# Attention of an encoder block in an order from estimated times, outputs of two query blocks at a time, the second norm's factor behind its product

## The chip, the cores and the metric

The kernel runs on one core of a Trainium2 chip. A core has five engines with a queue of instructions each: TensorE (PE) multiplies matrices into PSUM, VectorE (DVE), ScalarE (ACT) and GpSimd (POOL) do the elementwise work, SyncE (SP) issues DMAs. An engine takes its instructions in their order; semaphores hold one until what it needs is there. The metric is the time of one execution on the device in microseconds; the time before is the median of three runs.

## The reference

One layer on a sequence of 1024 frames with 1024 features, in float32:

```
h   = rmsnorm(x); q, k, v of groups A and B = split(h @ w_in)      # 8 heads of 64 each
ya  = softmax(q k^T / 8 + bias) v       # own chunk of 64 frames and the 8 before it
z   = q k^T / 8                         # group B: stick breaking, strictly causal
a   = exp(log_sigmoid(z) + sum of log(1 - sigmoid(z)) over the keys between)
yb  = a v
x   = x + concat(rmsnorm(ya), rmsnorm(yb)) @ w_out
x   = x + (silu(conv3(gate)) * conv3(value)) @ w_ffn_out            # gate|value = rmsnorm(x) @ w_ffn_in
out = rmsnorm(x)
```

## The kernel before

**Precision.** Each float32 operand of a large product is split into a high part and a low rest, and three products (high x high, high x low, low x high) are added in PSUM: `mm3` (L138 to L145). The split costs a cast on ACT and a subtraction on DVE or GpSimd.

**Stages.** From 0 to 58 us the input is normed and q, k and v of the first head pair are made. Attention of group B follows (58 to 355 us), then that of group A (355 to 540 us; the second half of the output projection begins inside it), the rest of that projection with the second norm's beginning (to 600 us), and the feed-forward part to the end. Heads go in pairs, n = 0 to 3 in group B and 4 to 7 in group A (there p = n - 4).

**Group B** (`BlockB`, L385 on). For each pair of heads and query block i of 128 frames there are KT - i key blocks; the order of frames is reversed, so block 0 is the widest with 8. `scores` writes z (`zb`) into one of two PSUM buffers of two banks each; two sigmoids on ACT, a scan and a product on DVE (L410 to L415) follow. `turn` transposes the result by key blocks (`tpb`, L423) and ACT copies it to SBUF. `output` (L433) multiplies by v with half of the array's columns per head, (`yb`), and DVE copies the sums (L437). Block b's scores, block b-2's transposes and an output in between make one turn of the loop (L667 to L701).

**Group A** (`BlockA`, L451 on) does the same with a softmax: bias (L482), maximum (L484), exponential with its sum (L492), reciprocal (L493), shares (L494), transposes (`tpa`), outputs (`yy`, L521), and a copy into a quarter of `yq`. Each four blocks the result is scaled and split for the output projection (L536, L537) and squared.

**The filler.** Projections of later head pairs (`q`, `k`, `v`) and the group B half of the output projection (`pb`) are a generator, whose pieces of three matmuls are put between the pieces of attention at fixed rates (RATE_B, RATES_A, `run`). Before the first block of a head pair, `need` finishes the projections it lacks.

**What sets the order.** The order on PE is the program's. On DVE, ACT, GpSimd and SP a scheduler puts the instructions in order by a simulated timeline until the second half of the output projection; from there on (`own_order`, `loads_order`, L843 to L846) these are in program order too. PSUM buffers in question: two banks `pj` for projections, two banks `med` for transposes, outputs and sums, two pairs `big` for scores.

**Second norm of attention.** The outputs of group B are spilled to memory as they are; their squares are summed, and `prepare_b` loads them again, multiplies by gain and factor (L547) and splits them for `pb`. The product is added to x directly (L577). For group A the factor is applied behind the product (`paf`, L575).

Of the kernel before, what the change touches and what calls it, by code (L numbers as in the profile page):

```python
# [8 lines left out]
F32 = mybir.dt.float32  # L9
# [6 lines left out]
P = 128  # L16
T = 1024
D = 1024
KT = 8
# [36 lines left out]
def tile_hybrid_block(  # L56
# [56 lines left out]
    first = one("first", "first", BF16)  # L113
    GP.memset(first, 0.0)
    GP.tensor_copy(first[:, :P], ident)
# [71 lines left out]
    with tc.tile_pool(name="kp", bufs=2) as kp:  # L187
# [19 lines left out]
        zero = kp.tile([P, 2 * GW], BF16, tag="tmp", name="zero")  # L207
# [61 lines left out]
        def project(ct, outs, name):  # L269
            wh, wl = weights(w_in[ct], name, lo_eng=GP)  # L270
            for g in range(G):
                for k in range(KT):
                    mm3(outs[g : g + 1], wh, wl, cols(k), hh[k], hl[k], k == 0, k == KT - 1, (g,))
                    yield 0.65

        def scaled(o, g, scale, name):
            f = kp.tile([P, GW], F32, tag="tmp", name=f"{name}_f{g}")
            V.scalar_tensor_tensor(
                out=f, in0=o, scalar=scale, in1=rb1[:, rows(g)], op0=ALU.mult, op1=ALU.mult
            )  # L280
            return f

        A, B = slice(0, 64), slice(64, 128)
        qk_of, v_of = {}, {}

        def stack_q(n, outs):
            s = 6 * (n % 2)
            qa, qb = slot(s, f"qa{n}", F32R), slot(s + 1, f"qb{n}", F32R)
            for g in range(G):
                f, r = scaled(outs[g], g, 0.125, f"q{n}"), rows(g)  # L290
                S.copy(qa[A, r], f[A, :])
                S.copy(qb[B, r], f[B, :])
                sub(qa[B, r], f[A, :], qa[A, r])
                sub(qb[A, r], f[B, :], qb[B, r])
                yield
            qk_of[n] = [qa, qb]

        def stack_k(n, outs):
# [3 lines left out]
            for g in range(G):  # L302
                f, r = scaled(outs[g], g, 1.0, f"k{n}"), rows(g)
                if n == 0:
                    for t, h in ((ka, A), (kb, B), (ka, B), (kb, A)):
                        S.copy(t[h, r], f[A if t is ka else B, :])
                    for t, h, l in ((ka, A, la), (kb, B, lb), (ka, B, la), (kb, A, lb)):
                        sub(l[h, r], f[A if t is ka else B, :], t[h, r])
                else:
                    GP.tensor_copy(ka[A, r], f[A, :])  # L310
                    GP.tensor_copy(kb[B, r], f[B, :])
                    nc.sync.dma_start(r32(ka[B, r]), r32(ka[A, r]))
                    nc.sync.dma_start(r32(kb[A, r]), r32(kb[B, r]))
                    sub(la[A, r], f[A, :], ka[A, r])
                    sub(lb[B, r], f[B, :], kb[B, r])
                    nc.sync.dma_start(r32(la[B, r]), r32(la[A, r]))
                    nc.sync.dma_start(r32(lb[A, r]), r32(lb[B, r]))
                yield
            qk_of[n] += [ka, kb, la, lb]

        def project_qk(n):
            base, p = (12, n) if n < 4 else (0, n - 4)
            for ct, what, stack in ((base + p, "q", stack_q), (base + 4 + p, "k", stack_k)):
                outs = [pj(f"{what}{n}_p{g}") for g in range(G)]
                wh, wl = weights(w_in[ct], f"{what}{n}", lo_eng=GP)
                st = stack(n, outs)
                steps = [(g, k) for g in range(G) for k in range(KT)]
                if n == 7 and what == "k":
                    steps = [(g, k) for ks in ((1, 4, 5, 6, 7), (0, 2, 3)) for g in range(G) for k in ks]
# [1248 lines left out]
```

## Time and profile before

| | us |
|---|---|
| median of three runs (1263.59 to 1266.56) | 1263.99 |
| the profiled execution | 1265.32 |
| its span, first to last instruction | 1263.5 |
| PE busy | 1234.6 |
| DVE busy | 967.3 |
| ACT busy | 655.2 |
| GpSimd busy | 332.6 |

The mean granted clock of TensorE is 0.993 of full speed. A matmul's end is modelled and neighbours overlap in the profile, so the time from one start to the next says what one costs, not its duration. The time that an engine spends idle, and what ended it, is told in the table of waits.

### The profile page before, as it was taken

Reading aid. Unit: us, or ns where it says so; the run is one execution under the profiler, and the core shown is the slowest. Engines: PE = TensorE matmul, PEld = TensorE weight load, DVE = VectorE, ACT = ScalarE, POOL = GpSimd, SP = SyncE. Lnnn points to the kernel's source line nnn. Section 1 sums busy time; section 2 is a strip of 40 time slices with the busy share of each in tenths; the row PEclk is TensorE's granted clock in tenths of the full one; section 3 lists DMA queues with packets and bytes.
Section 4 is the critical chain, followed back from the end, with each engine's and each line's share of the span. In section 5 each row is a group of like instructions: output and inputs, shape, how many; then the busy total and the mean of one; then the engine's idle time right before and its main releaser. Section 6 shows DMA issues by size and latency. Waiting matters only on the chain.

```text
span 1263.5 us, 17952 instructions
## 1 busy us (share of the span) xinstructions
PE 1234.6 (98%) x6936; PEld 1029.9 (82%) x6936; DVE 967.3 (77%) x1383; ACT 655.2 (52%) x1104; POOL 332.6 (26%) x236
## 2 busy tenths in 40 slices
PE   8999999999999999999999999999999999999996
PEld 6978888987897878878688888888888887888886
DVE  7766687677556697557699887887887879969885
ACT  6344656565577777733455444444444345444424
POOL 4211122121311122013001534433433422142034
PEclk9999999999999999999999999999999999999998
DMA  6111121112201262122222122122122096330003
GB/s 236 34 34 34 51 67 55 31 51 67 84 18 43 67 206 70 35 92 100 76 84 97 71 83 100 67 84 100 67 84 101 34 359 274 135 132 1 1 1 134
DMA packets 36869, 109.27 MB, mean 86 GB/s; under 512 B 4400, under 2 KB 7600, under 8 KB 36784
## 3 DMA queue, kind: packets, MB, share of 16 engines
q1 hardware_dynamic: 36640, 108.02, 24.8%
q8 instruction: 54, 0.88, 0.3%
q14 instruction: 31, 0.25, 0.1%
q10 hardware_dynamic: 144, 0.11, 0.1%
HBM read 78.75 MB, written 22.02 MB: 80 GB/s over the span
## 4 chain that ended last, share of the span: by engine, by line
PE 88%; DVE 6%; ACT 3%; DMA 2%; issue 1%; POOL 1%; SPq 0%; DVEq 0%; ACTq 0%; POOLq 0%
PE u_a L979 8%; PE u_e L979 8%; PE dz L1494 8%; PE v_p L365 7%; PE q_p L142 7%; PE k_p L142 6%; PE u_c L979 4%; PE u_d L979 4%; PE u_b L979 4%; PE u L1031 4%; PE dj L1494 3%; PE dm L1494 3%; PE pb L142 3%; PE yb L433 3%; PE tpb L423 2%; PE yy L521 2%
## 5 line engine op out<-in xcount | busy, mean ns | idle before, releaser
L412 DVE TENSOR_TENSOR_SCAN zb<-zb,first 128x1024 f32<-128x1024 f32 (+3 forms) x64 | 86.9, 1360 | 36.4 <-ACT zb L411 35.6
L365 PE MATMUL v_p<-v_h,hTh 128*128 128x256 f32 x256 | 74.5, 291 | 0.0
L1003 DVE SCALAR_TENSOR_TENSOR gt<-cg,cst,gt 128x1023 f32<-128x1023 f32 (+1 forms) x44 | 73.8, 1678 | 0.8
L365 PE MATMUL v_p<-v_l,hTh 128*128 128x256 f32 x256 | 72.3, 282 | 0.0
L365 PE MATMUL v_p<-v_h,hTl 128*128 128x256 f32 x256 | 72.3, 282 | 0.0
L424 ACT COPY tb<-tpb 128x512 f32<-128x512 f32 (+3 forms) x96 | 43.1, 481 | 55.8 <-PE tpb L423 55.4
L410 ACT ACTIVATE acts<-zb 128x1023 f32<-128x1023 f32 (+3 forms) x64 | 41.8, 653 | 48.2 <-PE zb L405 47.4
L869 POOL TENSOR_TENSOR up_r<-up_r 128x512 f32<-128x512 f32 x18 | 39.2, 2179 | 102.5 <-issue 92.5
L1003 DVE SCALAR_TENSOR_TENSOR vt<-cv,cst,vt 128x1023 f32<-128x1023 f32 (+1 forms) x44 | 57.7, 1312 | 1.5 <-ACT vt L997 0.7
L142 PE MATMUL q_p<-hTh,q_h 128*128 128x512 f32 x128 | 53.4, 426 | 2.3 <-ACT hTh L228 2.0
L142 PE MATMUL k_p<-hTh,k_h 128*128 128x512 f32 x128 | 54.0, 432 | 0.0
L997 ACT ACTIVATE vt<-cv,cst 128x1024 f32<-128x1024 f32 x22 | 27.4, 1245 | 45.9 <-DVE cv L872 45.9
L142 PE MATMUL q_p<-hTl,q_h 128*128 128x512 f32 x128 | 49.7, 398 | 0.7 <-DVE hTl L229 0.6
L494 ACT ACTIVATE pa<-pa,sta 128x640 f32<-128x640 f32 (+4 forms) x64 | 44.1, 695 | 12.0 <-DVE sta L493 11.8
L365 PEld LDWEIGHTS v_p<-v_h,hTh 128*128 128x128 f32 x256 | 48.8, 191 | 1.4 <-issue 1.0
L142 PE MATMUL k_p<-hTl,k_h 128*128 128x512 f32 x128 | 49.9, 400 | 0.0
L415 DVE TENSOR_TENSOR acts<-zb,acts 128x1023 f32<-128x1023 f32 (+3 forms) x64 | 48.1, 753 | 2.2
L142 PE MATMUL q_p<-hTh,q_l 128*128 128x512 f32 x128 | 49.4, 396 | 0.0
L142 PE MATMUL k_p<-hTh,k_l 128*128 128x512 f32 x128 | 49.3, 396 | 0.0
L492 ACT ACTIVATE pa<-sa,sta 128x640 f32<-128x640 f32 (+4 forms) x64 | 42.3, 661 | 13.4 <-DVE sta L484 8.8
L365 PEld LDWEIGHTS v_p<-v_h,hTl 128*128 128x128 f32 x256 | 48.9, 191 | 0.3
L365 PEld LDWEIGHTS v_p<-v_l,hTh 128*128 128x128 f32 x256 | 48.8, 191 | 0.0
(1264 smaller groups left out, 4031.3 us busy)
## 6 DMA issues: line engine op xcount, KB each, us to landing
up_r<-in_w_up_dram SPq DMA_DIRECT2D x44, 512.0 KB, 4.2
act<-vt SPq DMA_DIRECT2D x22, 512.0 KB, 2.6
dr<-in_w_dn_dram SPq DMA_DIRECT2D x20, 512.0 KB, 6.5
dr<-act SPq DMA_DIRECT2D x20, 512.0 KB, 7.2
k_r<-in_w_in_dram SPq DMA_DIRECT2D x8, 512.0 KB, 3.6
v_r<-in_w_v_dram SPq DMA_DIRECT2D x8, 512.0 KB, 3.9
x<-in_xT_dram SPq DMA_DIRECT2D x8, 512.0 KB, 4.5
x2d<-x SPq DMA_DIRECT2D x16, 256.0 KB, 2.0
```

The lines of the kernel that those rows point to most:

```text
L142: PE.matmul(o, w[:, sl], t[:, rows(g)], start=first and i == 0, stop=last and i == 2,)
L365: PE.matmul(ov, a[k][:, cols(t)], b[:, sl], start=k == 0 and i == 0 and t4 % 2 == 0, stop=k == KT - 1 and i == 2, skip_group_check=True,)
L410: S.activation(a[:, 1:w], z[:, 1:], AF.Sigmoid)
L412: V.tensor_tensor_scan(out=z, data0=z, data1=first[:, :w], initial=0.0, op0=ALU.mult, op1=ALU.add)
L415: V.tensor_tensor(out=a[:, 1:w], in0=z[:, : w - 1], in1=a[:, 1:w], op=ALU.mult)
L424: S.copy(at[:, b0 * P : (b0 + m) * P], tp[:, : m * P])
L492: S.activation(po, full, AF.Exp, bias=st[:, 0:1], accum_out=st[:, 1:2])
L494: S.activation(pr[:, : nk * P], pr[:, : nk * P], AF.Copy, scale=st[:, 2:3])
L979: PE.matmul(o, w[:, cols(k)], t, start=start and k == 0 and i == 0, stop=k == 3 and i == 2, skip_group_check=True,)
L1003: V.scalar_tensor_tensor(out=t[:, : T - lag], in0=o[:, lag:], scalar=c1(c + ct), in1=t[:, : T - lag], op0=ALU.mult, op1=ALU.add,)
L1031: PE.matmul(o, a[:, cols(k if r is None else r)], hp2[k][t][:, rows(g)], start=first and i == 0, stop=last and i == 2,)
L1494: PE.matmul(o[m], w[:, cols(m)], t, start=i in (0, 1, 4, 5) and p == ps_[0] and j == 0, stop=p == ps_[-1] and j == 2, skip_group_check=True,)
```

## The change

- The scheduler no longer orders DVE, ACT, GpSimd and SP in attention. A class `Flow` keeps a time for PE (`now`, advanced by `work` after each piece) and for each other engine, and chains of operations with estimated durations (`on_v`, `on_s`, `on_g`, `load`). As PE's time passes, the operation that could start first is put into the program. An L beside V or G stands for a resource that both hold. The order it results in is kept as it is.
- Before PE's code uses what a chain makes, or a PSUM bank whose last reader is a chain (`Banks`), `ready` takes pieces from the filler until the table says that the chain ends within 0.3 us.
- Outputs: both blocks of a pair in one bank, one after the other. In group B the pairs are a wide and a narrow block (ORDER_B now begins with the narrow one), in group A two neighbours; there one copy serves both.
- The shares of the first head of group A are multiplied on DVE, those of the second stay on ACT.
- At block 4 of head pairs 0 to 2 of group A, `need` finishes the next head pair's projections (before: at block 0 of that pair).
- The outputs of group B are scaled by the gain and split before they are spilled, as high and low parts; the norm's factor is applied behind the product (`scale` in `out_part`), as group A did.
- The halves of q, k and the products (`tmp`) have three buffers for two, the weights are fetched one ahead in an explicit list, and `first` is made when group B begins.

```diff
-ORDER_B = (0, 7, 1, 6, 2, 5, 3, 4)
+ORDER_B = (7, 0, 6, 1, 5, 2, 4, 3)
...
-RATE_B, LEAD_B = 32.0, 8.0
+RATE_B, LEAD_B = 31.0, 8.0
 RATES_A, LEAD_A = (25.0, 25.0, 25.0, 21.0), 6.5
+LAG = 0.25
+START = 8.0
+SLACK = 0.6
...
+                self.now, self.free, self.chains = 0.0, dict.fromkeys("VSGDL", 0.0), []
...
+            def add(self, *ops, after=(), behind=None, slack=0.0):
+                c = Chain(ops, self.now + LAG + slack, after, behind, slack)
+                self.chains.append(c)
+                return c
+            def start(self, c):
+                if c.behind and not c.behind.begun or not all(a.done for a in c.after):
+                    return None
+                return max([c.t] + [self.free[e] for e in c.ops[0][0]] + [a.t for a in c.after])
+            def step(self, limit=float("inf")):
+                best = None
+                for c in self.chains:
+                    t = self.start(c)
+                    if t is not None and t <= limit and (best is None or t < best[0]):
+                        best = t, c
+                if best is None:
+                    return False
+                t, c = best
+                engines, busy, wait, do = c.ops.pop(0)
+                do()
+                c.begun = True
+                for e in engines:
+                    self.free[e] = t + busy
+                c.t = t + busy + (wait if engines != "D" or not c.ops or c.ops[0][0] != "D" else 0)
+                c.t += c.slack if c.ops and engines[0] in "GD" else 0
+                if not c.ops:
+                    c.done = True
+                    self.chains.remove(c)
+                return True
...
+            def work(self, us):
+                self.now += us
+                while self.step(self.now):
+                    pass
...
+            def need(self, *chains):
+                self.emit(*chains)
+                self.now = max([self.now] + [c.t for c in chains])
...
+        def on_v(n, do, own="V"):
+            return own, n / 960 + 0.075, 0.09, do
+        def on_s(n, do):
+            return "S", n / 1200 + 0.1, 0.1, do
+        def on_g(n, do):
+            return "GL", n / 420 + 0.1, 0.1, do
+        def load(kb, do, us=2.2):
+            return "D", kb / 260, us, do
...
+            def chain(self, *ops, after=(), then=(), slack=SLACK):
+                head = flow.add(ops[0], after=[self.users[0], *after], behind=self.last)
+                rest = flow.add(*ops[1:], after=[head, *then], slack=slack)
+                self.users.popleft()
+                self.users.append(rest)
+                self.last = head
+                return head, rest
...
+            def get(self, name):
+                self.wait(*self.users.popleft())
+                mine = []
+                self.users.append(mine)
+                return self.make(name), mine
...
-                    S.copy(at[:, b0 * P : (b0 + m) * P], tp[:, : m * P])
...
+                    flow.work(0.109 * m)
+                    o = self.at[h][:, self.c0 + b0 * P : self.c0 + (b0 + m) * P]
+                    tp = tp[:, : m * P]
+                    mine.append(flow.add(on_s(m * P, lambda o=o, tp=tp: S.copy(o, tp))))
+                    self.turned += mine
+            def output(self, yy):
+                ready(*self.turned)
...
-                v, y = v_of[self.n], yb_of[self.n]
-                yy = med(f"y{self.nm}")
...
-                            yy[HS[h], :P], v[:, off : off + 64], self.at[h][:, cols(j)],
-                            start=j == 0, stop=j == nk - 1,
+                            yy[HS[h], :], v[:, off : off + 64],
+                            self.at[h][:, self.c0 + j * P : self.c0 + (j + 1) * P],
+                            start=j == 0, stop=j == nk - 1, skip_group_check=True,
                         )
-                V.tensor_copy(y[:, cols(i)], yy[:, :P])
+                flow.work(0.218 * nk + 0.15)
...
+                share = on_s(
+                    w + 60, lambda: S.activation(pr[:, :w], pr[:, :w], AF.Copy, scale=st[:, 2:3])
+                ) if h else on_v(w, lambda: V.tensor_scalar(
+                    out=pr[:, :w], in0=pr[:, :w], scalar1=st[:, 2:3], scalar2=None, op0=ALU.mult
+                ))
+                self.chain[h] = flow.add(
+                    on_v(2 * P + 100 * (nk == 5), mask),
+                    on_v(w, top),
+                    on_s(w + 170, lambda: S.activation(
+                        po, full, AF.Exp, bias=st[:, 0:1], accum_out=st[:, 1:2]
+                    )),
+                    on_v(8, lambda: V.reciprocal(st[:, 2:3], st[:, 1:2])),
+                    share,
+                    after=[bias_of[p][1]],
+                )
...
+                flow.work(0.218 * nk + 0.15)
...
-                y = kp.tile([P, GW], F32, tag="tmp", name=f"yb{i}_{g}")
-                nc.sync.dma_start(y, spill[i - 4][:, rows(g)])
-                gained(i, y, rbb, g)
+                def begin(i=i):
+                    for t, x in zip(spill[i - 4], (yh[i], yl[i])):
+                        nc.sync.dma_start(r32(x[:, r]), t[:, r])
+                yb_chains[i, g] = flow.add(load(512, begin), after=[spilled[i - 4]])
...
-            o = pj(f"{name}_{d}_{g}")
...
+                c = yb_chains.get((k, g))
+                for _ in range(40):
+                    if not c or c.done and c.t <= flow.now:
+                        break
+                    yield None
+                if c:
+                    flow.need(c)
                 off = (k - base) * 256 + (d % 2) * P
                 mm3([o], wh, wl, slice(off, off + P), yh[k], yl[k], k == base, k == base + 3, (g,))
+                flow.work(0.68)
...
-            if base == 0:
-                f = kp.tile([P, GW], F32, tag="tmp", name=f"{name}f_{d}_{g}")
-                V.tensor_tensor(out=f, in0=o, in1=rba[:, rows(g)], op=ALU.mult)
-                o = f
-            V.tensor_tensor(out=x2[d][:, rows(g)], in0=x2[d][:, rows(g)], in1=o, op=ALU.add)
...
+            def scale():
+                t["f"] = kp.tile([P, GW], F32, tag="tmp", name=f"{name}f_{d}_{g}", bufs=3)
+                V.tensor_tensor(out=t["f"], in0=o, in1=rb[:, rows(g)], op=ALU.mult)
+            first, rest = fs.chain(
+                on_v(GW, scale),
+                on_v(GW, lambda: V.tensor_tensor(out=x, in0=x, in1=t["f"], op=ALU.add), "VL"),
+                after=[rb_chains[g]], then=[x2_chains[d]], slack=0.0,
+            )
+            mine.append(first)
+            x2_chains[d, g] = rest
...
+        def ready(*chains):
+            for c in chains:
+                while not c.done or c.t > flow.now + 0.3:
+                    us = next(fill, None)
+                    if us is None:
+                        break
+                    done[0] += us
+            flow.need(*chains)
...
+                def low():
+                    V.scalar_tensor_tensor(
+                        out=tile_(1), in0=y[:, r], scalar=gain, in1=r32(t[0]),
+                        op0=ALU.mult, op1=ALU.subtract,
+                    )
+                def keep(i):
+                    return load(256, lambda: nc.sync.dma_start(spill[n][i][:, r], r32(t[i])))
+                hi, kept = fs.chain(
+                    on_s(GW, lambda: S.activation(tile_(0), y[:, r], AF.Copy, scale=gain)), keep(0),
+                    after=y_chains[n],
+                )
+                return [kept, fs.chain(on_v(GW, low, "VL"), keep(1), after=[hi])[1]]
+            parts = [half(r) for r in halves]
+            ops = [on_s(GW, lambda r=r: S.activation(y[:, r], y[:, r], AF.Square)) for r in halves]
+            if n:
+                ops.append(on_g(T, lambda: GP.tensor_tensor(out=yb_of[0], in0=yb_of[0], in1=y, op=ALU.add)))
+            spilled[n] = flow.add(*ops, after=sum(parts, []) + spilled[n - 1 : n], slack=SLACK)
...
-                    o = ending.pop(0)
-                    o.output()
...
+                    pair, ending = ending, []
+                    n = pair[0].n
+                    if pair[0].i == ORDER_B[0]:
+                        ready(*v_chains[n])
+                    yy, mine = meds.get(f"y{pair[0].nm}")
+                    for j, o in enumerate(pair):
+                        o.output(yy[:, cols(j)])
+                    mine.append(flow.add(*(
+                        on_v(P, lambda o=yb_of[n][:, cols(o.i)], j=cols(j), yy=yy: V.tensor_copy(o, yy[:, j]))
+                        for j, o in enumerate(pair)
+                    )))
+                    y_chains.setdefault(n, []).append(mine[0])
...
-                    u.turn(h)
-                    if h == 1:
-                        ending.append(u)
+                    k = units.index(u)
+                    u.turn(h, units[k ^ 1])
+                    if h == 1 and k % 2:
+                        ending = units[k - 1 : k + 1]
...
+            def copy():
+                if i % 4 == 1:
+                    yq_of[p] = kp.tile([P, GW], F32, tag="sq", name=f"yq{p}_{i}", bufs=1)
+                V.tensor_copy(yq_of[p][:, (i % 4 - 1) * P : (i % 4 + 1) * P], yy[:, : 2 * P])
+            c = flow.add(on_v(2 * P, copy), after=yq_chains)
...
                 at["qk"] = n - 1
                 need(n)
+                ready(*qk_chains[n])
+            if cur and cur.i == 4 and cur.p < 3:
+                need(cur.n + 1)
...
+                if ending and h == 0 and ending.i % 2:
+                    if ending.i == 1:
+                        ready(*v_chains[ending.n])
+                    if ending.p == 3 and ending.i == 5:
                         add_last(0)
-                    ending.output()
+                    yy, mine = meds.get(f"yy{ending.p}_{ending.i}")
+                    for j in range(2):
+                        blocks[b - 3 + j].output(yy[:, cols(j)])
...
-                loads_order = tc.manual_schedule(engines={nc.sync.engine})
-                loads_order.__enter__()
-                own_order = tc.manual_schedule(engines={V.engine, S.engine, GP.engine})
-                own_order.__enter__()
             for d in range(KT):
+                if g == 0 and d % 2 == 0:
```

Three places in the new order follow. Names carry the head pair p, the block and the head: `sa1_4_0` are the scores of head pair 1, block 4, head 0; `k6`, `q7` are projections of n = 6 and 7.

PE at block 4 of head pair 1 in group A. Before:

```order
L477 MATMUL sa1_4_0_4209<-ka5_3194,qa5_3075 128x512
L478 MATMUL sa1_4_0_4209<-la5_3196,qa5_3075 128x512
L142 MATMUL k6_p1_4003<-hTh7_178,k6_h_4006 128x512
L142 MATMUL k6_p1_4003<-hTl7_179,k6_h_4006 128x512
L142 MATMUL k6_p1_4003<-hTh7_178,k6_l_4007 128x512
L142 MATMUL q7_p0_4232<-hTh0_116,q7_h_4236 128x512
L142 MATMUL q7_p0_4232<-hTl0_117,q7_h_4236 128x512
L142 MATMUL q7_p0_4232<-hTh0_116,q7_l_4237 128x512
L521 MATMUL yy1_2_4243<-pta1_2_4167,v5_2133 64x128 x10
L504 MATMUL tpa1_3_0_4256<-ident_68,pa1_3_0_4145 128x128 x4
```

Now:

```order
L143 MATMUL k6_p1_4179<-hTh7_175,k6_l_3917 128x512
L709 MATMUL sa1_4_0_4211<-ka5_3211,qa5_3087 128x512
L710 MATMUL sa1_4_0_4211<-la5_3213,qa5_3087 128x512
L761 MATMUL tpa1_3_0_4220<-ident_68,pa1_3_0_4060 128x128 x4
L709 MATMUL sa1_4_1_4229<-kb5_3212,qb5_3088 128x512
L710 MATMUL sa1_4_1_4229<-lb5_3214,qb5_3088 128x512
L761 MATMUL tpa1_3_1_4237<-ident_68,pa1_3_1_4115 128x128 x4
L143 MATMUL q7_p0_4242<-hTh0_113,q7_h_4140 128x512
```

The 48 matmuls of `k6`, of which the first row is the last, all stand ahead of block 4, and projections have gone from between its two heads.

PE at the outputs of blocks 2 and 3 of the same head pair. Before, block 3's alone, block 2's having come earlier:

```order
L142 MATMUL q7_p0_4232<-hTh4_154,q7_l_4237 128x512
L521 MATMUL yy1_3_4304<-pta1_3_4255,v5_2133 64x128 x10
L504 MATMUL tpa1_4_0_4323<-ident_68,pa1_4_0_4215 128x128 x4
L142 MATMUL q7_p0_4232<-hTh5_162,q7_h_4236 128x512
L142 MATMUL q7_p0_4232<-hTl5_163,q7_h_4236 128x512
```

Now:

```order
L709 MATMUL sa1_5_0_4265<-ka5_3211,qa5_3087 128x384
L710 MATMUL sa1_5_0_4265<-la5_3213,qa5_3087 128x384
L774 MATMUL yy1_3_4272<-pta1_2_4097,v5_2118 64x128 x10
L774 MATMUL yy1_3_4272<-pta1_3_4219,v5_2118 64x128 x10
L761 MATMUL tpa1_4_0_4305<-ident_68,pa1_4_0_4218 128x128 x4
L709 MATMUL sa1_5_1_4313<-kb5_3212,qb5_3088 128x384
L710 MATMUL sa1_5_1_4313<-lb5_3214,qb5_3088 128x384
```

The outputs of the two blocks stand together and go to one bank.

ACT at block 4 of the same head pair (L492 and L740 are the exponential, L494 and L733 the shares, L505, L510 and L765 copies of transposes). Before:

```order
L492 ACTIVATE pa1_4_0_4215,sta1_4_0_4213<-sa1_4_0_4209,sta1_4_0_4213 128x512
L494 ACTIVATE pa1_4_0_4215<-pa1_4_0_4215,sta1_4_0_4213 128x512
L505 COPY pta1_3_4255<-tpa1_3_0_4256 128x512
L505 COPY pta1_3_4255<-tpa1_3_1_4278 128x512
L492 ACTIVATE pa1_4_1_4271,sta1_4_1_4269<-sa1_4_1_4265,sta1_4_1_4269 128x512
L510 COPY pta1_3_4255<-tpa1_3_2_4284 128x256
L494 ACTIVATE pa1_4_1_4271<-pa1_4_1_4271,sta1_4_1_4269 128x512
L492 ACTIVATE pa1_5_0_4297,sta1_5_0_4295<-sa1_5_0_4291,sta1_5_0_4295 128x384
```

Now:

```order
L740 ACTIVATE pa1_4_0_4218,sta1_4_0_4217<-sa1_4_0_4211,sta1_4_0_4217 128x512
L765 COPY pta1_3_4219<-tpa1_3_1_4237 128x512
L740 ACTIVATE pa1_4_1_4236,sta1_4_1_4235<-sa1_4_1_4229,sta1_4_1_4235 128x512
L765 COPY pta1_3_4219<-tpa1_3_2_4252 128x256
L733 ACTIVATE pa1_4_1_4236<-pa1_4_1_4236,sta1_4_1_4235 128x512
L740 ACTIVATE pa1_5_0_4271,sta1_5_0_4270<-sa1_5_0_4265,sta1_5_0_4270 128x384
L765 COPY pta1_4_4304<-tpa1_4_0_4305 128x512
```

The share of head 0 has gone to DVE; the copies stand between the exponentials.

## Rows read from the trace of the kernel before

**Rows 1.** The page, part 1: busy us (share of the span) xinstructions of each engine.

```profile
PE 1234.6 (98%) x6936; PEld 1029.9 (82%) x6936; DVE 967.3 (77%) x1383; ACT 655.2 (52%) x1104; POOL 332.6 (26%) x236
```

**Rows 2.** Windows: us; busy us (xinstructions) by engine; PEclk; DMA share, GB/s.

```profile
58.00:355.00 297.00, 290.18 (x2105) 247.12 (x2103) 204.77 (x291) 165.00 (x287) 54.30 (x37) 0.99 0.18 51
355.00:512.00 157.00, 153.25 (x1103) 126.30 (x1104) 111.11 (x265) 119.26 (x250) 30.57 (x24) 1.00 0.27 82
512.00:600.00 88.00, 86.94 (x498) 70.92 (x495) 54.92 (x99) 40.73 (x79) 16.60 (x12) 1.00 0.23 79
```

**Rows 3.** Waits of PE from 58 to 355 us: us in total, times, longest.

```profile
PE zb L404 <- DVE acts L415: 3.7, 2, 2.2
PE tpb L423 <- ACT tb L424: 1.7, 3, 0.7
PE yb L433 <- ACT tb L424: 0.9, 2, 0.7
PE tpb L423 <- DVE y L437: 0.4, 1, 0.4
```

**Rows 4.** Waits of PE from 355 to 512 us, the two largest of six.

```profile
PE nb_rb L172 <- ACT pta L505: 1.1, 1, 1.1
PE pb L142 <- DVE x L577: 1.0, 2, 0.5
...
```

**Rows 5.** Timeline of PE (start us, us, operation, idle time before it); one window.

```profile
76.46 0.40 PE L142 MATMUL k_p<-hTl,k_h 128*128 128x512 f32 x1
76.69 0.40 PE L142 MATMUL k_p<-hTh,k_l 128*128 128x512 f32 x1
79.29 0.64 PE L404 MATMUL zb<-ka,qa 128*128 128x512 f32 x1 [2.20 <-DVE acts L415]
...
82.92 0.39 PE L142 MATMUL k_p<-hTh,k_l 128*128 128x512 f32 x1
...
80.00:85.00 5.00, 5.00 (x23) 4.20 (x23) 2.09 (x2) 2.89 (x4) 0.00 (x0) 0.71 0.00 0
```

**Rows 6.** Timeline of PE around two runs of outputs.

```profile
424.46 0.39 PE L142 MATMUL q_p<-hTh,q_l 128*128 128x512 f32 x1
424.78 1.31 PE L521 MATMUL yy<-pta,v 128*64 128x128 f32 x20
426.02 0.66 PE L504 MATMUL tpa<-ident,pa 128*128 128x128 f32 x4
...
434.11 0.88 PE L521 MATMUL yy<-pta,v 128*64 128x128 f32 x12
434.92 0.44 PE L504 MATMUL tpa<-ident,pa 128*128 128x128 f32 x2
```

**Rows 7.** Windows of blocks 4 to 7 of head pairs 1 and 3.

```profile
417.00:436.00 19.00, 19.00 (x148) 15.44 (x147) 11.96 (x31) 15.11 (x36) 4.84 (x4) 1.00 0.20 55
518.00:540.00 22.00, 22.00 (x175) 18.08 (x175) 13.22 (x38) 16.07 (x41) 0.00 (x0) 1.00 0.08 25
```

**Rows 8.** Groups by form on ACT, 26 to 600 us: the shares.

```profile
L494 ACT ACTIVATE pa<-pa,sta 128x512 f32<-128x512 f32 x8 | 5.8, 722 | 1.7 <-DVE sta L493 1.7
L494 ACT ACTIVATE pa<-pa,sta 128x384 f32<-128x384 f32 x8 | 4.9, 613 | 1.4 <-DVE sta L493 1.4
L494 ACT ACTIVATE pa<-pa,sta 128x256 f32<-128x256 f32 x8 | 4.0, 506 | 0.2 <-DVE sta L493 0.2
L494 ACT ACTIVATE pa<-pa,sta 128x128 f32<-128x128 f32 x8 | 3.2, 399 | 1.4 <-DVE sta L493 1.4
```

**Rows 9.** One line: tensor_scalar of DVE within SBUF.

```profile
L443 DVE TENSOR_SCALAR bias<-bias,cst x8: 340/344/355, 32.6 to 439.9; 128x256 f32<-128x256 f32 x8
```

**Rows 10.** Timeline of DVE beside GpSimd; then that line of DVE.

```profile
442.55 2.40 POOL L120 TENSOR_TENSOR wob_l<-wob_r,wob_h 128x1024 fp32r<-128x1024 f32 x1 [2.10 <-ACT wob_h L123]
442.68 2.82 DVE L547 SCALAR_TENSOR_TENSOR yb<-yb,cst,rbb 128x512 f32<-128x512 f32 x1
...
L547 DVE SCALAR_TENSOR_TENSOR yb<-yb,cst,rbb x8: 747/752/2822, 442.7 to 474.8; 128x512 f32<-128x512 f32 x8
```

**Rows 11.** A group of DVE: half of the projection, multiplied by its factor.

```profile
L575 DVE TENSOR_TENSOR paf<-pa,rba 128x512 f32<-128x512 f32 x16 | 11.0, 688 | 8.0 <-PE pa L142 7.8
```

More of the change, by code (lines that the diff above doesn't have):

```diff
@@ L1 @@
+from collections import deque
 from contextlib import ExitStack, contextmanager
@@ L267, in tile_hybrid_block, with __init__ @@
         pre[1] = preload(w_v[1], "v0_1", "wb", kp, ("x10", "x11"), 1)
[L269 to L277, printed above, removed]
+        class Chain:
+            def __init__(self, ops, t, after, behind, slack):
+                self.ops, self.t, self.behind, self.slack = list(ops), t, behind, slack
+                self.after = [a for a in after if a]
+                self.begun = self.done = False
@@ new lines, in tile_hybrid_block, with __init__, emit, drain @@
+        class Flow:
+            def __init__(self):
+                self.now, self.free, self.chains = 0.0, dict.fromkeys("VSGDL", 0.0), []
[31 more added lines that the diff above has]
+                    pass
+            def emit(self, *chains):
+                for c in chains:
+                    while not c.done:
+                        if not self.step():
+                            raise RuntimeError("a chain waits for what never comes")
+            def need(self, *chains):
+                self.emit(*chains)
+                self.now = max([self.now] + [c.t for c in chains])
+            def drain(self):
+                while self.step():
+                    pass
@@ L278, in scaled, with take @@
+        load_next([])
+        def take(queue=w_ready):
+            t, c = queue.popleft()
+            flow.need(c)
+            return t["h"], t["l"]
+        def scaled(o, g, scale, name, t):
+            t["f"] = kp.tile([P, GW], F32, tag="tmp", name=f"{name}_f{g}", bufs=3)
             V.scalar_tensor_tensor(
-                out=f, in0=o, scalar=scale, in1=rb1[:, rows(g)], op0=ALU.mult, op1=ALU.mult
+                out=t["f"], in0=o, scalar=scale, in1=rb1[:, rows(g)], op0=ALU.mult, op1=ALU.mult
@@ L321, in project_qk @@
+            for g in range(G):
+                yield half(g)
         def project_qk(n):
[L322 to L325, printed above, removed]
+            qk_chains[n] = []
+            for what, stack in (("q", stack_q), ("k", stack_k)):
+                wh, wl = take()
+                outs, mine = [None] * G, [None] * G
@@ L348, in project_qk, with stacked @@
                         yield None
-                next(st, None)
+        def stacked(n, st, mine, ready, count):
+            g = sum(c == KT for c in count) - ready
+            first, rest = next(st)
+            mine[g].append(first)
+            qk_chains[n].append(rest)
         def project_v(n):
-            u0 = 2 * (n // 2)
-            us = [pre[i] if n == 0 else weights(w_v[u0 + i], f"v{n}_{i}", lo_eng=GP) for i in range(2)]
+            us = pre if n == 0 else [take()]
+            v_chains[n] = v_chains[n + 1] = []
             for i in range(2):
```

488 lines of the change are left out of this document (316 added, 172 removed).

## The prediction

> **What bounds the kernel now.** I read the page's first part before anything else. TensorE (PE) is busy for 1234.6 of 1263.5 us [rows 1], so the change can give back only what PE loses now: idle time, a lowered clock, and time lost between matmuls, which the busy figure hides. The table of windows then says where it idles: 6.8 us in group B (58 to 355 us), 3.75 in group A (355 to 512), 1.06 in the half projection that follows [rows 2]. From 630 us on the change touches nothing. DVE and ACT are at 69% and 56% in group B, 71% and 76% in group A [rows 2], so for PE they matter only where they come in bursts. The waits of PE name the causes. In group B they are score banks not yet released (3.7 us in two waits), transposes whose bank ACT had not emptied (1.7) or DVE (0.4), and outputs whose transposes ACT had not copied (0.9): 6.7 in all [rows 3]. In group A it is a handful of waits of about one microsecond or less, the largest on ACT [rows 4]. The timeline shows what one long wait costs besides itself. PE stood still for 2.2 us, and the matmuls behind it ran at 0.43 us from start to start where 0.227 is usual, the five microseconds at a mean clock of 0.71, between the levels of 2.4 and 1.2 GHz [rows 5]. From 79.29 to 82.92 us, 3.63 us passed for seven matmuls of 512 and two of 384 columns, 7 x 0.227 + 2 x 0.174 = 1.94 us at full clock: 1.7 us lost.
>
> **The change part by part.** PE issues the same matmuls (6353 rows of the same sizes in both orders), so no term comes from their number.
>
> *Outputs of two blocks.* The outputs use half the array's columns. A run of 20 takes 1.24 us to the next start, a run of 12 takes 0.81 [rows 6]: 0.054 each, and 0.16 per run that does not depend on its length. Getting in costs 0.32 - 0.227 = 0.09 more [rows 6]. So each run costs 0.25 us beyond its matmuls. Before there are 64 runs (32 per group), in the new order 34 (one pair is split by a projection): 30 x 0.25 = **-7.5 us**, on the path, because PE itself is late by it. Bounds: 0, if the cost is another one that stays, and 64 x 0.25 = 16.
>
> *Order of group B.* The program now asks its table whether a chain is done before it writes a score, a transposition or an output, and takes projections from the filler as long as it is not. Of today's loss, 6.7 us of waits and 1.7 of clock, all could go: 8.4. What can return is a fault in the table. It takes 0.218 us per key block plus 0.15 per output; by the rows above two matmuls of 0.054 take 0.108. For a pair of nine key blocks it counts 2.26 us, PE needs 9 x 0.108 + 0.25 = 1.22. So at each of the 16 pairs of group B the table is 1.0 us ahead of PE and may think a chain done that is not. Bounds of what returns: 0 and 16 x 1.0. I take three waits of 0.8 us, the mean of today's eight [rows 3], as most chains have more slack than one microsecond: 2.4, all too short for the clock to fall. Term: -8.4 + 2.4 = **-6.0**.
>
> *Order of group A.* Here the new order is tighter. Before block 4 of head pair 1 the projection of the next head pair is finished in one piece of 48 matmuls, and what was pulled early is then missing. From the first score of block 4 to that of the next head pair PE now spends 19.0 us and is never idle, ACT being busy for 15.1 and DVE for 12.0 [rows 7]. In the new order PE's work there is 21 projection matmuls (4.8 us), scores 2.5, 28 transposes at 0.109 (3.05), 34 output matmuls at 0.054 (1.85), two runs at 0.25: 12.7. ACT loses half of the shares, 0.72 + 0.61 + 0.51 + 0.40 = 2.24 [rows 8], and a cast of 0.6: 12.3 us, 97% of PE's stretch. DVE loses two q or k scalings and a subtraction (2.1), and gains four shares: a bias of 256 columns in SBUF took 0.344 [rows 9], which bounds the 1280 columns of four shares between 4 x 0.344 = 1.4 (if width costs little) and 1.7 (in proportion); I take 1.5: 11.4 us. Today no wait appears with ACT at 80% [rows 7]. If that is what a chain across three engines can hold, the stretch takes 12.3 / 0.8 = 15.4, a wait of 2.7; if it could hold 97%, nothing. I take 2.0. Head pair 3 has PE work of 15.2 us against 16.1 - 2.2 = 13.9 of ACT [rows 7]: 1.5 by the same rule. Head pairs 0 and 2 keep 16 and 19 us of PE work and cost nothing. Of today's 3.8 us the order covers half, which leaves 1.9. Group A thus goes from 3.8 to 5.4: **+1.6**. Bounds: -3.8 and, with both stretches at 80% and nothing covered, 2.7 + 2.2 = +4.9.
>
> *Factor of the second norm.* Eight scalings leave DVE, 0.75 us each and up to 2.82 [rows 10], with eight subtractions and eight casts of ACT. Eight subtractions and eight copies of ACT come instead in group B, and 16 multiplications of 0.69 us [rows 11] in group A and behind it. All of it lies beside PE: DVE is at 71% there and at 62% behind it [rows 2], and the third buffer of the scaled halves gives the late multiplication room. SP gets 16 stores where it had 4 and 16 loads where it had 8, of half the size. Cost 0; without that cover the 16 multiplications would be 11 us of DVE, of which at most the last two (1.4) stand before the first norm. The queues of DVE, ACT, GpSimd and SP, now in program order through the whole of attention, are the ones on which the waits above fall.
>
> *Beginning and end.* PE's order is the same up to the first projection of head pair 1. The first wide score now comes 45 projection matmuls later, the last output about 11 us of projections earlier; PE has work in both places: 0.
>
> Sum, against the profiled execution: 1265.3 - 7.5 - 6.0 + 1.6 = 1253.4. It lies 1.3 us above the median of the runs, 1264.0. Forecast: **1252.1 us**.
>
> **A rule against the change.** One scaling of DVE took 2.82 us instead of 0.75 while GpSimd subtracted for 2.40 us beside it [rows 10]. The Trainium skill says why, in "SBUF — State Buffer", section "Who interferes with whom": DVE and GpSimd share one pair of ports as an exclusive lock, held for a whole instruction, by DVE operations with two inputs in SBUF, and also by a tensor_scalar within SBUF in its two-port mode. The trace agrees on the first kind; no row shows the second. The table lets no instruction marked L overlap GpSimd, but the 32 new shares of DVE are not marked.
>
> **The rivals.**
> - Every wait goes: -7.5 - 8.4 - 3.8 - 1.1 = -20.8, so 1244.5 by the profile and 1243.2 as a median. For it: the filler is pulled whenever the table doubts. Against it: the 97% above.
> - The waits only change place, and the runs of outputs alone are gained: 1265.3 - 7.5 - 1.3 = 1256.5. For it: before is also ordered from estimates, and lost only 13 us in 540.
> - The shares collide with GpSimd (by that rule): GpSimd is busy 30.6 of 157 us in group A [rows 2], so 6 of 32 shares meet it and wait half of 2.4 us each, 7.5 us of DVE in all. If all reached PE, 1252.1 + 7.5 = 1259.6; if one in four does, 1254.0.
> - Slower: the output's price. If the table's 1.0 us of excess became a wait at each of the 32 pairs, 32 us would come while 7.5 + 13.3 (all waits and the clock of today) go: 1265.3 + 11.2 - 1.3 = 1275.2. It decides from 21 of the 32 pairs on. For it: the excess is certain. Against it: a chain has to end just within that microsecond, and each wait brings PE's count back in line.
>
> **How the numbers follow.** Chances: forecast 0.43, every wait gone 0.20, runs alone 0.20, collisions 0.07, output's price 0.10. A change of 0.3%, 3.8 us, is about what a measurement of this kernel can tell from none. Faster (below 1260.2): nearly all of the forecast and of the first rival, three quarters of the second, most of the third, 0.81. Within 0.3%: the rest of these, 0.10. Slower: most of the last, 0.09. The range reaches from 1241 (every wait gone, and a little on the runs) to 1263 (runs alone, with half of the clock and collisions against it); the tenth above and some hundredths below are left out.
>
> **What would show it.** Right: 34 runs of outputs with the next start 0.16 us late, as now; PE's idle time in group B at 2 to 3 us and no stretch at the lower clock; in blocks 4 to 7 of head pairs 1 and 3 waits of PE on ACT or DVE, 1 to 2 us in all at each. Wrong: waits of transposes just behind most pairs of outputs (the table's price), shares of DVE longer than 1 us beside GpSimd (the ports), or PE waiting behind 540 us, where I expect nothing. I am wrong in the mechanism if PE's idle time falls and the span does not.

## The result and the profile after

The changed kernel takes 1245.89 us (median of 4 runs, 1245.05 to 1247.4) beside 1264.38 for the kernel before in the same runs: ratio 0.9852, 95% interval 0.9835 to 0.9869. Run once more beside later versions it took 1246.32 (0.9852, 0.9838 to 0.9866). The forecast was 1252.1: right in its sign and inside its range, 6 us too slow. The profiled execution took 1247.4 us with a span of 1245.6.

Page, part 1 of the changed kernel, and the windows of group B, group A and the half projection, each over its new place (columns as in [rows 1, 2]):

```profile
PE 1221.6 (98%) x6936; PEld 1031.8 (83%) x6936; DVE 975.6 (78%) x1403; ACT 633.8 (51%) x1072; POOL 342.1 (27%) x240
```

```profile
65.00:313.00 248.00, 247.34 (x1864) 215.57 (x1863) 188.68 (x254) 154.27 (x272) 46.77 (x33) 1.00 0.21 61
313.00:512.00 199.00, 195.09 (x1493) 170.69 (x1492) 147.41 (x356) 127.70 (x278) 39.74 (x33) 1.00 0.29 84
512.00:580.00 68.00, 67.20 (x316) 55.20 (x313) 42.26 (x60) 21.24 (x32) 25.03 (x15) 1.00 0.32 109
```

PE loses 0.7 us in group B where it lost 6.8, and the clock stands at 1.00 there. In group A it loses 3.9. PE's waits, in group B and then in group A (us in total, times, longest), beside [rows 3, 4]:

```profile
PE yb L659 <- ACT tb L649: 0.4, 1, 0.4
PE tpb L645 <- DVE y L1033: 0.2, 1, 0.2
```

```profile
PE tpa L761 <- ACT pta L765: 2.3, 7, 0.6
PE v_p L558 <- DVE k_f L435: 0.7, 1, 0.7
PE yy L774 <- ACT pta L765: 0.6, 1, 0.6
PE tpa L761 <- DVE yq L1069: 0.3, 1, 0.3
```

The score banks, 3.7 us in [rows 3], are gone from the list. A pair of outputs in group B, first on PE, then what DVE does meanwhile (start, us, operation):

```profile
176.22 0.39 PE L143 MATMUL q_p<-hTh,q_l 128*128 128x512 f32 x1
176.54 2.19 PE L659 MATMUL yb<-tb,v 128*64 128x128 f32 x36
178.65 0.50 PE L143 MATMUL q_p<-hTh,q_h 128*128 128x512 f32 x1
178.99 0.39 PE L143 MATMUL q_p<-hTl,q_h 128*128 128x512 f32 x1
179.22 0.39 PE L143 MATMUL q_p<-hTh,q_l 128*128 128x512 f32 x1
179.45 0.60 PE L645 MATMUL tpb<-ident,acts 128*128 128x128 f32 x4
179.81 0.49 PE L143 MATMUL q_p<-hTh,q_h 128*128 128x512 f32 x1
180.13 0.39 PE L143 MATMUL q_p<-hTl,q_h 128*128 128x512 f32 x1
```

```profile
178.46 0.69 DVE L121 TENSOR_TENSOR lb<-k_f,kb 64x512 fp32r<-64x512 f32 x1
179.18 0.69 DVE L625 TENSOR_TENSOR acts<-zb,acts 128x511 f32<-128x511 f32 x1
179.78 0.48 DVE L1033 COPY y<-yb 128x128 f32<-128x128 f32 x2
```

Starts on PE are 0.32 us apart into the run (0.227 is usual), 2.11 over its 36 matmuls (36 x 0.054 = 1.95, and 0.16), and then there is something that the prediction did not have: the first projection behind the run takes 0.34 to the next start, the second 0.23 again. (Behind the four transposes a projection takes 0.32 too, but there nothing is lost: it starts 0.03 us behind the last transpose, where 0.109 is usual.)

The same rows show what the prediction misread. The pair has nine key blocks, and its run is 36 rows: four for each key block, since each of the two matmuls that the program writes for one (a float32 call with 64 columns) is two rows of the trace. With 0.09 into the run PE needs 2.20 us for the pair. The table counts 2.26.

Added up from start to start over PE's matmuls (a gap above 0.1 us is a wait, and counts with what the matmul ahead of it took beyond its usual spacing, so that these waits are larger than in the lists), the two profiles differ by:

| us | before | after |
|---|---|---|
| into and out of runs of outputs (64, 34) | 15.3 | 8.1 |
| first matmul behind such a run | 5.2 | 2.3 |
| waits in group B | 8.0 | 0.9 |
| lower clock in group B | 1.7 | 0 |
| waits in group A | 4.9 | 5.5 |

That is -18.3; the two profiled executions are 17.9 us apart.

### The profile page after: what moved, and what is told of

Read it like the earlier page. It is cut to its first block, busy times and chain, and to the rows that moved or that the text cites. A ratio compares the mean times of both kernels' runs of the same rounds, so it can differ in the third digit from the quotient of the medians.

```text
span 1245.6 us, 18039 instructions
## 1 busy us (share of the span) xinstructions
PE 1221.6 (98%) x6936; PEld 1031.8 (83%) x6936; DVE 975.6 (78%) x1403; ACT 633.8 (51%) x1072; POOL 342.1 (27%) x240
## 4 chain that ended last, share of the span: by engine, by line
PE 83%; DVE 9%; ACT 4%; issue 2%; POOL 1%; DMA 1%; SPq 0%; DVEq 0%; ACTq 0%; POOLq 0%
PE u_a L1364 8%; PE u_e L1364 8%; PE dz L1879 8%; PE v_p L558 7%; PE q_p L143 6%; PE k_p L143 6%; PE u_c L1364 4%; PE u_b L1364 4%; PE u_d L1364 4%; PE pb L143 3%; PE dm L1879 3%; PE dj L1879 3%; PE pa L143 3%; PE yb L659 2%; PE tpb L645 2%; PE yy L774 2%
## 5 line engine op out<-in xcount | busy, mean ns | idle before, releaser
L622 DVE TENSOR_TENSOR_SCAN zb<-zb,first 128x128 f32<-128x128 f32 (+3 forms) x64 | 86.7, 1360 | 40.9 <-ACT zb L618 40.4
L617 ACT ACTIVATE acts<-zb 128x127 f32<-128x127 f32 (+3 forms) x64 | 42.1, 658 | 43.6 <-PE zb L609 43.2
L740 ACT ACTIVATE pa<-sa,sta 128x640 f32<-128x640 f32 (+4 forms) x64 | 42.3, 662 | 22.4 <-DVE sta L726 17.8
L121 POOL TENSOR_TENSOR q_l<-q_r,q_h 128x1024 fp32r<-128x1024 f32 x7 | 16.7, 2391 | 132.8 <-ACT q_h L416 132.8
L143 PE MATMUL k_p<-hTh,k_h 128*128 128x512 f32 x128 | 51.2, 410 | 0.0
L625 DVE TENSOR_TENSOR acts<-zb,acts 128x127 f32<-128x127 f32 (+3 forms) x64 | 47.4, 749 | 1.2
```

Of the source, the lines that this page charges most:

```text
L143: PE.matmul(o, w[:, sl], t[:, rows(g)], start=first and i == 0, stop=last and i == 2,)
L617: S.activation(a[:, 1:w], z[:, 1:], AF.Sigmoid)
L622: on_v(2 * w + 70, lambda: V.tensor_tensor_scan(out=z, data0=z, data1=first[:, :w], initial=0.0, op0=ALU.mult, op1=ALU.add)),
L625: on_v(w, lambda: V.tensor_tensor(out=a[:, 1:w], in0=z[:, : w - 1], in1=a[:, 1:w], op=ALU.mult)),
L740: on_s(w + 170, lambda: S.activation(po, full, AF.Exp, bias=st[:, 0:1], accum_out=st[:, 1:2])),
```

## The experiments

Each is an edit of the changed kernel, but for the second, which edits the kernel before. Ratios are to the kernel before, run beside it.

**Broken runs of outputs.** A projection between the two outputs of a pair; in the second kernel one more in the middle of each output. (In both, two tiles of the output weights come in exchanged places; sizes and numbers of instructions stay.)

```
 for j, o in enumerate(pair):
     o.output(yy[:, cols(j)])
+    if j == 0: done[0] += next(fill, None) or 0.0     # and alike in group A
```

> One projection is put between the two outputs of each pair, so that the run of output matmuls is broken: 64 runs as in the kernel before, instead of 34; everything else is ordered by the same rules. Theory (a run of half-array matmuls costs 0.25 us beyond its matmuls): 30 runs x 0.25 = 7.5 us more than 1245.9, so 1253.4, PE's idle time unchanged. Rival (the pairs are worth nothing by themselves, the gain is all in fewer waits): 1245 to 1247.

> As with single outputs, but each output is broken once more by a projection in its middle: 114 runs of output matmuls instead of 34. Theory (0.25 us per run): 80 x 0.25 = 20.0 us more than 1245.9, so 1265.9. Rival A (no price per run): 1245 to 1248. Rival B (the price is not per run but per output, that is, per bank released): the same as with 64 runs.

Measured: 1255.47 us (0.9926, 0.9913 to 0.9938) and 1278.14 (1.0105, 1.0091 to 1.0119). So 30 more runs cost 9.6 us and 80 more 32.3: 0.32 and 0.40 each, above the 0.25 that I held for the price, and far from nothing. The rest is in the first matmul behind a run. Over all runs of the first kernel the way in costs 0.097 us and the way out 0.148, as forecast; and the first matmul behind takes 0.111 longer if it is a projection of 512 columns (26 runs), 0.103 with 256 (8), 0.056 if it is a transpose (30). 0.245 and 0.11 make 0.355. PE's waits in the first kernel are no more than in the changed one (group A 3.5 us, group B none); the second has 4.9 us more in group B and 4.1 less in group A.

**The pairs alone, in the kernel before.** Both outputs of a pair in one bank, with the buffer of transposes that a pair needs; nothing else of the change.

```
-o = ending.pop(0); o.output()
+yy = med(...)
+for j, o in enumerate(pair): o.output(yy[:, cols(j)])
+for j, o in enumerate(pair): V.tensor_copy(y[:, cols(o.i)], yy[:, cols(j)])
```

> The kernel before with outputs of two blocks at a time and nothing else of the change: 32 runs of output matmuls instead of 64, the order of scores, transposes and projections as it was, the other engines ordered by the scheduler. Theory A (0.3 us or more per run saved, as the broken runs showed, whatever the order around them): 32 x 0.32 = 10 us less than 1264.8, so 1255, PE's waits as before. Theory B (an output that waits for its mate's transposes comes late in this order, and new waits eat half): 1259 to 1262.

Measured: 1279.13 us (1.0107, 1.0093 to 1.0121), 14 us slower than before. Both theories fail, the second in size. Into and out of 32 runs goes 8.0 us, so the saving is there; the waits ate it three times over, 22.2 us in group B (8.0 before) and 11.8 in group A (4.9). PE's waits in group B, then one of them on DVE and on PE:

```profile
PE tpb L430 <- DVE y L697: 14.0, 14, 1.7
PE zb L404 <- DVE acts L415: 4.7, 4, 2.2
PE tpb L430 <- ACT tb L431: 0.3, 1, 0.3
```

```profile
205.21 2.30 DVE L412 TENSOR_TENSOR_SCAN zb<-zb,first 128x1024 f32<-128x1024 f32 x1 [1.19 <-ACT zb L411]
207.42 0.46 DVE L697 COPY y<-yb 128x128 f32<-128x128 f32 x2
```

```profile
204.78 0.28 PE L439 MATMUL yb<-tb,v 128*64 128x128 f32 x2
...
208.03 0.63 PE L430 MATMUL tpb<-ident,acts 128*128 128x128 f32 x4 [1.64 <-DVE y L697]
```

The pair ends just before 204.99. At 205.21 DVE starts a scan of 1024 columns, and only behind it copies the outputs out. The bank is one of two that the transposes need, so PE waits 1.64 us. The scheduler put the scan ahead of them. In the changed kernel, above, only the rest of a subtraction and a product of 0.69 us stand ahead of the copies, and PE's transposes go on without a wait. Whether putting these copies first would mend this kernel was not tried.

**The order of the other engines.** PE's order as in the changed kernel (its 6936 rows come in the same order in both traces); DVE, ACT, GpSimd and SP are left to the scheduler through attention.

```
-loads_order = tc.manual_schedule(engines={nc.sync.engine}); loads_order.__enter__()
-own_order = tc.manual_schedule(engines={V.engine, S.engine, GP.engine}); own_order.__enter__()
     # both entered later instead, at the second half of the output projection
```

> PE's order is the changed kernel's, instruction by instruction; SP, DVE, ACT and GpSimd are ordered by the scheduler through attention, as in the kernel before, and not by the program. Theory A (PE's order alone removes the waits of group B): 1245 to 1248. Theory B (the order of the other engines is what keeps the chains on time): PE's waits of 6 to 8 us in group B come back, and with long ones the lower clock: 1252 to 1256.

Measured: 1268.06 us (11 runs; 1.0022, 1.0013 to 1.0031): 22 us slower than the changed kernel, more than the theory with the larger number asked for, and slower than before. PE's largest waits, in group B (first line) and group A, then one of the first on DVE and on PE:

```profile
PE zb L608 <- DVE acts L625: 5.8, 9, 1.4
```

```profile
PE tpa L761 <- DVE yq L1065: 3.4, 2, 1.9
PE tpa L761 <- DVE pa L734: 3.0, 3, 2.2
PE tpa L761 <- ACT pa L733: 2.5, 5, 0.8
```

```profile
255.12 2.61 DVE L622 TENSOR_TENSOR_SCAN zb<-zb,first 128x1024 f32<-128x1024 f32 x2 [2.42 <-ACT zb L618]
257.64 1.10 DVE L571 TENSOR_SCALAR v<-v_p,rn 128x128 f32<-128x128 f32 x4
258.66 1.41 DVE L625 TENSOR_TENSOR acts<-zb,acts 128x1023 f32<-128x1023 f32 x2
```

```profile
258.16 0.33 PE L645 MATMUL tpb<-ident,acts 128*128 128x128 f32 x1
259.93 0.50 PE L608 MATMUL zb<-kb,qb 128*128 128x512 f32 x1 [1.44 <-DVE acts L625]
```

DVE takes four scalings of v, 1.10 us, ahead of the product on which the next score waits; without them the wait of 1.44 would be about 0.3. The wait of 2.2 us in group A stands behind two loads of ACT's tables (1.28 us each, from 525.23), which the changed kernel does not have there. All waits together are 8.8 us in group B (0.9) and 14.7 in group A (5.5).

**The output's price in the table.**

```
-flow.work(0.218 * nk + 0.15)
+flow.work(0.108 * nk + 0.15)
```

> The table counts 0.108 us per key block of an output plus 0.15, what PE needs, instead of 0.218 plus 0.15. Theory of the prediction (the excess of 1.0 us per pair makes the table think chains done that are not, and PE waits): PE's waits in the two groups, about 6 us in all, fall by 2 to 3, so 1243 to 1244. Rival A (the excess does no harm, since every pull from the filler and every wait brings the count back in line): 1245 to 1247. Rival B (the excess is what keeps chains from being called done too late, projections are now pulled too early and missing later): 1248 to 1251, with waits in the second half of a head pair.

This edit does not put the price right. As the rows of the pair above show, PE needs 4 x 0.0545 = 0.218 us per key block, what the table had; the edit halves it. At each pair of nine key blocks the table now falls 0.9 us behind PE; it was not 1.0 us ahead before.

Measured: 1244.51 us (0.9839, 0.9826 to 0.9853), 1.4 to 1.8 below the changed kernel, inside both intervals. Gaps above 0.1 us cost 1.0 us in group B (0.9 in the changed kernel) and 1.9 in group A (5.5 in both profiles of the changed kernel). But in group B PE also waits for times too short for that list, because the modelled end of the matmul ahead covers them. One of them, on PE and on DVE:

```profile
292.91 0.40 PE L143 MATMUL q_p<-hTh,q_l 128*128 128x512 f32 x1
293.38 0.50 PE L608 MATMUL zb<-kb,qb 128*128 128x512 f32 x1
```

```profile
292.65 0.68 DVE L625 TENSOR_TENSOR acts<-zb,acts 128x511 f32<-128x511 f32 x1
```

The score starts 0.05 us behind the product that frees its bank, and 0.47 us behind the projection instead of 0.23. Such starts, late by more than 0.05 us, number 15 in group B with the halved price, 2.4 us in all, and 4 with 0.7 us in the changed kernel. So the halved price costs some 1.7 us in group B; in group A fewer waits came with it, and why was not shown.

**ACT's load in group A.** All shares on ACT again.

```
-share = on_s(...) if h else on_v(...)
+share = on_s(...)
```

> All shares of group A on ACT again (64 there, none on DVE), the table told so; the rest as in the changed kernel. Theory of the prediction (a chain across three engines holds ACT at 80% of PE's work): in blocks 4 to 7 of head pair 1 ACT goes from 11.7 to about 13.9 us beside 15.4 of PE, and alike in head pair 3; PE's waits in group A grow by 3 to 4, so 1249 to 1250. Rival (in program order the chain holds up to 95%): 1245.5 to 1247.

Measured: 1244.58 us (0.9837, 0.9823 to 0.985): no slower, and PE's waits in group A are 2.4 us instead of 5.5. Blocks 4 to 7 of head pair 1 in the changed kernel (402.1 to 417.8 us) and in this one (400.9 to 415.9), answering to [rows 7] (the fourth and fifth figures behind the length are DVE and ACT):

```profile
402.00:418.00 16.00, 15.44 (x136) 12.92 (x135) 13.00 (x33) 11.71 (x28) 4.94 (x4) 1.00 0.31 76
```

```profile
401.00:416.00 15.00, 14.92 (x135) 12.72 (x133) 11.58 (x28) 13.47 (x32) 5.21 (x4) 1.00 0.28 72
```

With ACT at 13.47 of 15 us, 90%, PE has no gap above 0.1 us in these blocks, and is busier than with ACT at 73%. A limit of 80% does not exist here, and moving the shares to DVE earned nothing.

**No bunch before block 4, and shares kept off GpSimd.** Two kernels.

```
-if cur and cur.i == 4 and cur.p < 3: need(cur.n + 1)
```

```
-on_v(w, share)
+on_v(w, share, "VL")
```

> The rule that finishes the next head pair's projections before block 4 of a head pair is left out. Theory of the prediction (the bunch takes away the projections that blocks 4 to 7 would need): PE's waits there go, 1 to 2 us in all, so 1244 to 1245. Rival (the q and k halves are then late at the head pair's first score): 1247 to 1250, with waits of PE at the first scores of head pairs 1 to 3.

> The 32 shares of DVE are marked so that the table lets none of them overlap GpSimd's work. In the changed kernel three of them took 1.1 to 1.6 us instead of 0.3 to 0.5. Theory A (the collisions cost about 3 us of DVE and never reach PE): 1245 to 1247, and no share longer than 0.7 us. Theory B (they reach PE): PE's waits in group A fall by 1 to 2, so 1244 to 1245. Rival C (the table now holds shares back for GpSimd work that is not there in fact, and chains end later): 1247 to 1249.

Measured: 1243.66 us (0.9837, 0.9823 to 0.985) and 1244.67 (0.9841, 0.9828 to 0.9855). PE's waits in group A are 3.6 and 3.4 us instead of 5.5, and no late q or k shows without the bunch. The mark did not do all it should: one of the 32 shares still took 1.53 us, since the table's times are not the chip's. Neither difference stands clear of the intervals alone. Since every edit so far of how group A is ordered lowered its waits (to 1.9, 2.4, 3.6 and 3.4 us), these runs do not single out a rule that caused them.

**The norm's factor.**

```
-first, rest = fs.chain(on_v(GW, scale), on_v(GW, add, "VL"), ...)
+rest = flow.add(on_v(GW, add_from_psum), after=[x2_chains[d]])      # group B's half only
```

> The factor of the second norm is left out of the products of group B's half of the output projection: the product is added to x directly, 16 multiplications of 0.69 us and their buffers are gone, and that factor is missing in the result. Theory (the multiplications lie beside PE): 1245 to 1247. Rival (they reach PE, in group A or in the 67 us behind it, where DVE is the busiest of the three): 5 us less, 1241.

Measured: 1245.58 us (0.9848, 0.9835 to 0.9862), beside 1245.89: nothing, as forecast.

**Together.** The halved price, bunch and mark; and the halved price and bunch with all shares on ACT.

> Three edits of the rules together: the output's true price, no bunch before block 4, the 32 shares of DVE kept off GpSimd's work. Theory A (each takes its own waits of group A away: 1.4, 2.2 and 1.2 us): 1241 to 1242. Theory B (each merely deals the same few waits anew): 1243 to 1245, PE's idle time in group A again 2 to 4 us.

> The output's true price and no bunch, and all shares of group A on ACT, where they cannot meet GpSimd. Theory A (ACT has room, and DVE is relieved): 1241 to 1242. Theory B (only the deal of waits differs): 1243 to 1245.

> The changed kernel once more, beside the versions that it is compared with: 1245 to 1247.

Measured: 1243.40 us (0.9827, 0.9814 to 0.9841), 1244.04 (0.9834, 0.9821 to 0.9848), and 1246.32 for the changed kernel beside them. The first is the fastest of all, some 3 us under the changed kernel by medians, their intervals overlapping. PE's waits in both groups of the first, and its shares on DVE (ns min/median/max):

```profile
PE yb L659 <- ACT tb L649: 0.4, 1, 0.4
PE tpa L761 <- ACT pta L765: 0.3, 1, 0.3
PE zb L608 <- DVE acts L625: 0.2, 1, 0.2
```

```profile
L734 DVE TENSOR_SCALAR pa<-pa,sta x32: 278/515/555, 322.2 to 505.5; 128x640 f32<-128x640 f32 x16, 128x512 f32<-128x512 f32 x4, 128x384 f32<-128x384 f32 x4, 128x256 f32<-128x256 f32 x4
```

0.9 us of listed waits are left in 444. Taking 5 us of them away brought 3: matmuls of group B are 2.2 us farther apart than in the changed kernel, at full clock. Most of that is the 15 short waits that came with the halved price, here 2.4 us instead of 0.7 as well. So by group A's waits theory A is right, and by its time theory B. The two edits of group A without the halved price were not run together. Nor were the third buffers, the list of weights and the new ORDER_B varied by themselves.

## Why the prediction was right, and where it was not

- **Outputs, -7.5.** The sign and the path were right, the size was short: "each run costs 0.25 us beyond its matmuls". The way in and out measured 0.245, 30 x 0.245 = 7.4, so this part was right. The first matmul behind had to be counted too: before, 24 runs were followed by a projection of 512 columns, 6 by one of 256 and 34 by transposes, after 7, 0 and 27, and that is the 2.9 us of the table. About 10 in all; breaking the pairs gave 9.6.
- **"On the path, because PE itself is late by it".** True in the changed order, false as a property of the pairs: alone they cost 14 us. The sum added terms that depend on each other. It came out because the change has both.
- **Group B, -6.0.** The step that failed is the excess of 1.0 us per pair, for which "three waits of 0.8 us" were to return. "Two matmuls of 0.054 take 0.108" per key block takes a matmul of the program for a row of the trace: [rows 6] have a block of five key blocks as 20 rows, four to a key block. A pair of nine takes 2.20 us where the table counts 2.26, so the table was right and there was no excess. 0.6 came back by the list of waits, and the term was about -8.8 (7.1 of waits, 1.7 of clock).
- **Group A, +1.6.** Measured +0.6, and not where I put it: the gaps above 0.1 us in blocks 4 to 7 come to 0.6 us in head pair 1 instead of 2.0, to 0.4 in head pair 3 instead of 1.5. Two steps failed. The first is the same miscount, in "34 output matmuls at 0.054 (1.85)". The stretch has 68 such rows:

```profile
406.63 2.40 PE L774 MATMUL yy<-pta,v 128*64 128x128 f32 x40
415.02 1.75 PE L774 MATMUL yy<-pta,v 128*64 128x128 f32 x28
```

  That is 3.7 us, and without its waits the stretch took 14.9 us on PE instead of 12.7. ACT's 11.7 are 79% of that, not 97%, so the case that was priced did not come up. The second is the rule of 80% itself: with all shares on ACT 90% cost nothing. Head pair 2 has 2.0 and head pair 0 has 0.9 in all their blocks, where I gave nothing; what rule would have spared them is open, as said above.
- **Norm's factor, beginning and end, 0.** Right for the factor by its own experiment. PE's waits behind 579 us are some 2 us more than before; they differ as much between kernels that have the same code there, so no term follows.
- **The rule on the ports.** "No row shows the second kind": one of after does, first GpSimd, then DVE.

```profile
450.93 2.39 POOL L121 TENSOR_TENSOR wo_l<-wo_r,wo_h 128x1024 fp32r<-128x1024 f32 x1
```

```profile
452.01 1.59 DVE L734 TENSOR_SCALAR pa<-pa,sta 128x512 f32<-128x512 f32 x1
```

  The share, 0.48 us alone, ends 0.28 behind GpSimd's subtraction. This agrees with what the Trainium skill says in "SBUF — State Buffer", section "Who interferes with whom", on a tensor_scalar in the two-port mode. Three of 32 shares met GpSimd, 2.9 us of DVE in all, where I priced six and 7.5; one transpose waited 0.2 us for a share. The rival's size fails, its mechanism holds.
- **The rivals.** By its time, "every wait goes" (1243.2) lay nearer than the forecast: it was right on group B and wrong on group A, whose waits stayed, and by luck the outputs gave 2.6 us more than it counted. "Runs alone" fails as a mechanism, since neither the pairs without the order nor PE's order without that of the others is faster than before. "The output's price" falls with its premise: "the excess is certain" is the miscount. Halving the price moved the time by 1.4 us.

## What to carry to other kernels

A saving on the bottleneck engine is worth what the order of its partners lets through: the same pairs were worth -9.6 us in one order and +14 in another, so such terms are to be priced with the banks that they hold longer, and what the releasing engine has queued ahead. Price a change of operand shape over three matmuls, into, out of and first behind, and before a price per row goes into a sum, check how many rows of the trace one call of the program makes. A busy share of a partner engine is no limit by itself; look for what stands ahead in its queue when the chain is due.

## What the chip showed that was not expected

The first matmul of full width behind a run of half-array matmuls takes 0.11 us longer to the next start, beside the 0.15 at the change itself; a transpose takes 0.056 longer. Each float32 matmul with 64 columns is two rows of the trace, 0.054 us each, while a transpose or a product of split parts is one. A tensor_scalar of DVE within SBUF costs 0.29 us for 128 columns and 0.55 for 640 where it meets nothing, half a nanosecond per column.
